# Split weights of a phase's first three units: general-pool buffers in pieces of 512 columns

## The chip, the cores and the metric

One core of a Trainium2 chip runs the whole kernel. The metric is the device time of one execution in microseconds (us); smaller is better.

## The reference, cut to what matters

Two layers of an encoder, 256 tokens, width 2048, float32. Each layer has a mixing phase and a feed-forward phase, each between two norms:

```
for l in range(DEPTH):                                   # DEPTH = 2
    h = rmsnorm(x, pre_mix_norm)
    proj = h @ w_in                                      # 2048 -> q/kv latents, conv, delta-net inputs
    o_a = attention(...);  o_b = convolution module(...);  o_c = gated delta net, both directions(...)
    x = x + rmsnorm(concat(o_a, o_b, o_c) @ w_out, post_mix_norm)
    h = rmsnorm(x, pre_ffn_norm)
    f = (silu(h @ w_gate) * (h @ w_up)) @ w_down         # 2048 -> 5632 -> 2048
    x = x + rmsnorm(f, post_ffn_norm)
```

All weights are read from memory once, some 400 MB, and nearly all the arithmetic is in the products with them.

## The kernel before, in words

**Products in three parts.** A float32 operand is split into a rounded half `hi` and the rest `lo = x - hi`, and a product is three matmuls: hi·hi, lo·hi, hi·lo. `hilo` (L327 to L329) makes the split: the cast on ScalarE (ACT, L328) and the subtraction on VectorE (DVE, L329). Both the tokens (on the left, moved into TensorE as 128x128 blocks) and the weights (on the right, 512 columns wide) are split.

**Units.** `dense` (L337) forms a product of 256 tokens, as two halves t = 0 and t = 1 of 128, with a weight block of `n` columns. Its weight rows come in units of two chunks of 128 rows. `unit(u)` loads 128x1024 floats into a buffer `ws` (5 of them, `WSB`), takes a pair of buffers `wh`, `wl` (5 pairs, `WHB`) and splits all 1024 columns with one cast and one subtraction. A unit has 6 matmuls for t = 0 (L353, L354, L355 for each chunk) and 6 for t = 1.

**Phase starts.** Each of the four phases (mixing and feed-forward, in two layers) begins with a `dense` call that has `head=HEADG=3`: the block "gq" of the mixing phase and the first gate block in `first_block`. Its tokens come from the phase's new `x`, which the end of the phase before makes last. So the first three units run their t = 0 matmuls alone, are kept in `held`, and their t = 1 matmuls follow together after unit 2. Until then the three pairs `wh`, `wl` are in use. A phase ends in `out_proj`, whose last `dense` has `tail=TAILG=4`: the last four units run t = 0 first, then t = 1, so that the sum, the norm and the residual of t = 0 (L1201, L1204, L1205, `rsqrt_sum` L257 to L270, four additions L495) run beside the t = 1 matmuls. These four units hold four of the five pairs.

**New tokens.** `norm_quad` transposes four 128x128 blocks of `x` on TensorE (L439, 32 transposes for both halves) and splits the result; the first group of t = 0 goes through `hilo_col` in four steps (L332, L333), the others through L448 and `hilo`.

**Order.** The program text is not the order of the queues. A planner places the instructions: it gives each engine, as soon as its model of that engine is free, the ready instruction that stands earliest in the text. Ready means that its inputs are there and that the buffer for its output is free. So an instruction that stands late in the text is put ahead of an earlier one that is still waiting. `hold` (L112, L492 to L497) limits that for the head units: the subtractions of units 1 and 2 may not be put ahead of the residual of t = 0 (`issue_after` orders within one engine, here VectorE; at the very first start the engine is ScalarE for units 1 and 2). It says nothing on units 3 and up.

**Pools.** `U()` gives a 128x512 buffer from the general pool (64 of them, `UB`), which holds all token data.

Of the kernel before, what the change touches and what calls it, by code (L numbers as in the profile page):

```python
# [10 lines left out]
F32R = mybir.dt.float32r  # L11
# [5 lines left out]
P = 128  # L17
# [25 lines left out]
WHB = 5  # L43
# [10 lines left out]
def kernel(  # L54
# [12 lines left out]
    wpool = ctx.enter_context(tc.tile_pool(name="wpool", bufs=3))  # L67
# [5 lines left out]
    def U(dt=F32):  # L73
        return upool.tile([P, 512], dt, tag="u", name="u")
# [252 lines left out]
    def hilo(hi, lo, src):  # L327
        act.copy(out=hi, in_=src)  # L328
        dve.tensor_tensor(out=lo, in0=src, in1=hi.bitcast(F32), op=ALU.subtract)  # L329
# [7 lines left out]
    def dense(lhs, ks, n, load, evac, ch=2, need=None, pre=None, head=0, mid=None, tail=0,  # L337
              after0=None):

        acc = [psa.tile([P, 512], F32, tag="acc", name="acc") for _ in range(NT)]
        nu = -(-len(ks) // ch)
        held = []

        def mm(t, c, u, kc, wh, wl):
            i = u * ch + c
            rh = wh[:, c * n:(c + 1) * n]
            rl = wl[:, c * n:(c + 1) * n]  # L350
            xh, xl = lhs(kc[c], t)
            o = acc[t][:, 0:n]
            pe.matmul(o, xh, rh, start=(i == 0), stop=False)  # L353
            pe.matmul(o, xl, rh, start=False, stop=False)  # L354
            pe.matmul(o, xh, rl, start=False, stop=(i == len(ks) - 1))  # L355

        def unit(u):
            kc = ks[u * ch:(u + 1) * ch]
            m = len(kc)
            ws = wpool.tile([P, 1024], F32, tag="ws", name="ws", bufs=WSB)  # L360
            wv = ws[:, 0:m * n].rearrange("p (c n) -> p c n", c=m)
            load(wv, kc[0], m)
            wh = wpool.tile([P, 1024], F32R, tag="wh", name="wh", bufs=WHB)
            wl = wpool.tile([P, 1024], F32R, tag="wl", name="wl", bufs=WHB)
            with ExitStack() as order:
                if u < head:
                    for u0, ins in hold:
                        if u >= u0:
                            order.enter_context(tc.issue_after(ins.ins))
                hilo(wh[:, 0:m * n], wl[:, 0:m * n], ws[:, 0:m * n])  # L370
            if need is not None:
                for k in kc:
                    bg.ensure(*need(k))
            return u, kc, wh, wl

        for u in range(nu):
            a = unit(u)
            if head <= u < nu - tail:
                for c in range(len(a[1])):
                    for t in range(NT):  # L380
                        mm(t, c, *a)
            else:
                for c in range(len(a[1])):
                    mm(0, c, *a)
                held.append(a)
                if u == head - 1 and mid is not None:
                    mid()
                if u == nu - 1:
                    if pre is not None:
                        pre()  # L390
                        pre = None
                    evac(0, acc[0][:, 0:n])
                if u in (head - 1, nu - 1):
                    for h in held:
                        for c in range(len(h[1])):
                            mm(1, c, *h)
                    held.clear()
            bg.step(BUDGET)
        if pre is not None:
            pre()  # L400
        if after0 is not None:
            after0()
        for t in range(1 if tail else 0, NT):
            evac(t, acc[t][:, 0:n])
# [1056 lines left out]
```

## Time and profile before

| what | value |
|---|---|
| median of 3 runs | 2233.1 us (2231.53 to 2233.45) |
| profiled execution, its own time | 2234.73 us |
| its span in the trace | 2233.0 us |
| mean granted TensorE clock | 0.998 of full speed |
| TensorE (PE) busy | 99% of the span |
| VectorE (DVE) busy | 79% |
| ScalarE (ACT) busy | 53% |

The profiled execution lies 1.6 us above the median, and 1.7 us of its time lie outside the span. Busy shares of PE count a matmul up to its modelled end, so waits of PE are read from the starts of successive instructions and not from the busy share.

### The profile page before, as it was taken

Reading aid. Unit: us, or ns where it says so; the run is one execution under the profiler, and the core shown is the slowest. Engines: PE = TensorE matmul, PEld = TensorE weight load, DVE = VectorE, ACT = ScalarE, POOL = GpSimd, SP = SyncE. Lnnn points to the kernel's source line nnn. Section 1 sums busy time; section 2 is a strip of 40 time slices with the busy share of each in tenths; the row PEclk is TensorE's granted clock in tenths of the full one; section 3 lists DMA queues with packets and bytes.
Section 4 is the critical chain, followed back from the end, with each engine's and each line's share of the span. In section 5 each row is a group of like instructions: output and inputs, shape, how many; then the busy total and the mean of one; then the engine's idle time right before and its main releaser. Section 6 shows DMA issues by size and latency. Waiting matters only on the chain.

```text
span 2233.0 us, 29215 instructions
## 1 busy us (share of the span) xinstructions
PE 2203.0 (99%) x10483; PEld 1839.3 (82%) x10483; DVE 1762.0 (79%) x2873; ACT 1182.5 (53%) x1642; POOL 45.9 (2%) x93
## 2 busy tenths in 40 slices
PE   8999999999999999999999999999999999999998
PEld 7988887788888888888879888877888888888886
DVE  6777998899999897544486779979999998975444
ACT  6665545555555555444356655455555555554432
POOL 2000000000000000000000000000000000000000
PEclk9999999999999999999999999999999999999999
DMA  7554525546656656555556545245565566665553
GB/s 254 171 178 146 188 89 162 162 164 207 217 181 217 225 189 223 171 195 192 179 172 186 183 142 171 97 153 161 188 207 208 191 215 214 202 214 178 191 196 124
DMA packets 218545, 407.75 MB, mean 183 GB/s; under 512 B 17607, under 2 KB 30065, under 8 KB 218400
## 3 DMA queue, kind: packets, MB, share of 16 engines
q1 hardware_dynamic: 215360, 397.72, 54.3%
q0 software_dynamic: 3008, 8.16, 1.3%
q8 instruction: 82, 1.34, 0.2%
q14 instruction: 63, 0.52, 0.1%
q10 hardware_dynamic: 32, 0.01, 0.0%
HBM read 402.94 MB, written 2.90 MB: 182 GB/s over the span
## 4 chain that ended last, share of the span: by engine, by line
PE 92%; DVE 5%; DMA 1%; issue 0%; ACT 0%; SPq 0%; DVEq 0%; ACTq 0%; POOLq 0%
PE acc L1306 19%; PE tp L1306 19%; PE acc L353 16%; PE acc L354 16%; PE acc L355 16%; DVE wl L329 1%; DVE xs L495 1%; PE tp L1230 1%; PE tp L1051 1%; DVE u L950 1%; DMA cd<-u 1%; PE tp L795 0%; PE tp L802 0%; PE tp L1022 0%; DMA xs<-in_x_dram 0%
## 5 line engine op out<-in xcount | busy, mean ns | idle before, releaser
L328 ACT CAST wh<-ws 128x1024 fp32r<-128x1024 f32 (+3 forms) x820 | 815.5, 1010 | 795.2 <-PE acc L354 409.6
L329 DVE TENSOR_TENSOR wl<-ws,wh 128x1024 fp32r<-128x1024 f32 (+3 forms) x820 | 942.1, 1170 | 336.2 <-ACT wh L328 332.2
L353 PE MATMUL acc<-wh,u 128*128 128x512 f32 (+2 forms) x1792 | 695.5, 389 | 0.4
L354 PE MATMUL acc<-wh,u 128*128 128x512 f32 (+2 forms) x1792 | 686.2, 383 | 3.5 <-DVE u L329 1.8
L355 PE MATMUL acc<-wl,u 128*128 128x512 f32 (+2 forms) x1792 | 685.6, 383 | 3.0 <-DVE wl L329 3.0
L354 PEld LDWEIGHTS acc<-wh,u 128*128 128x128 f32 x1792 | 337.5, 188 | 68.4 <-DVE u L333 4.1
L355 PEld LDWEIGHTS acc<-wl,u 128*128 128x128 f32 x1792 | 336.8, 188 | 68.1 <-DVE wl L329 5.8
L353 PEld LDWEIGHTS acc<-wh,u 128*128 128x128 f32 x1792 | 337.3, 188 | 62.3 <-ACT u L332 2.5
L1306 PE MATMUL acc<-wh,u 128*128 128x512 f32 x1220 | 376.4, 389 | 0.0
L1306 PE MATMUL tp<-wh,u 128*128 128x512 f32 x1220 | 375.8, 389 | 0.0
L1306 PEld LDWEIGHTS acc<-wh,u 128*128 128x128 f32 x1220 | 228.7, 188 | 47.9 <-DVE u L329 0.6
L1306 PEld LDWEIGHTS tp<-wh,u 128*128 128x128 f32 x1220 | 228.9, 188 | 47.6
L1306 PE MATMUL acc<-wl,u 128*128 128x512 f32 x610 | 237.4, 389 | 0.0
L1306 PE MATMUL tp<-wl,u 128*128 128x512 f32 x610 | 237.3, 389 | 0.0
L1306 PEld LDWEIGHTS acc<-wl,u 128*128 128x128 f32 x610 | 114.5, 188 | 23.7
L1306 PEld LDWEIGHTS tp<-wl,u 128*128 128x128 f32 x610 | 114.5, 188 | 23.7
L950 DVE SCALAR_TENSOR_TENSOR u<-u,cols 128x241 f32<-128x241 f32 (+14 forms) x240 | 101.0, 470 | 0.0
L1344 ACT CAST wh<-ws 128x1024 fp32r<-128x1024 f32 x60 | 63.0, 1050 | 28.4 <-PE tp L1306 12.8
L1345 DVE TENSOR_TENSOR wl<-ws,wh 128x512 fp32r<-128x512 f32 x60 | 41.1, 686 | 23.8 <-ACT wh L1344 21.8
L328 ACT CAST u<-u 128x512 fp32r<-128x512 f32 (+2 forms) x48 | 27.8, 587 | 38.2 <-DVE u L448 34.2
L1329 ACT ACTIVATE u<-u,sm 128x512 f32<-128x512 f32 x40 | 28.8, 724 | 34.6 <-DVE u L1376 24.4
L1351 DVE TENSOR_TENSOR ws<-ws 128x512 f32<-128x512 f32 x60 | 41.5, 692 | 2.0
(303 smaller groups left out, 1541.8 us busy)
## 6 DMA issues: line engine op xcount, KB each, us to landing
ws<-in_w_gate_dram SPq DMA_DIRECT2D x176, 512.0 KB, 5.0
ws<-in_w_up_dram SPq DMA_DIRECT2D x176, 512.0 KB, 4.8
ws<-in_w_down_dram SPq DMA_DIRECT2D x176, 512.0 KB, 3.6
ws<-in_w_in_dram SPq DMA_DIRECT2D x112, 512.0 KB, 4.3
ws<-in_w_out_dram SPq DMA_DIRECT2D x64, 512.0 KB, 3.7
ws<-in_w_ukv_dram SPq DMA_DIRECT2D x16, 512.0 KB, 3.7
ws<-in_w_uq_dram SPq DMA_DIRECT2D x16, 384.0 KB, 3.5
ws<-in_w_in_dram SPq DMA_DIRECT2D x10, 444.0 KB, 4.1
```

Of the source, the lines that this page charges most:

```text
L328: act.copy(out=hi, in_=src)
L329: dve.tensor_tensor(out=lo, in0=src, in1=hi.bitcast(F32), op=ALU.subtract)
L353: pe.matmul(o, xh, rh, start=(i == 0), stop=False)
L354: pe.matmul(o, xl, rh, start=False, stop=False)
L355: pe.matmul(o, xh, rl, start=False, stop=(i == len(ks) - 1))
L495: ins = dve.scalar_tensor_tensor(out=xv, in0=parts[(c, t)], scalar=r[:, 0:1], in1=xv, op0=ALU.mult, op1=ALU.add)
L950: dve.scalar_tensor_tensor(out=o, in0=i, scalar=wc, in1=o, op0=ALU.mult, op1=ALU.add)
L1306: pe.matmul(o, a, b, start=count[i] == 1, stop=count[i] == total[i])
L1329: act.activation(out=sg[t], in_=x, func=AF.Silu, scale=rfb[0][:, t:t + 1])
L1344: act.copy(out=wh, in_=wg)
L1345: dve.tensor_tensor(out=wl[:, 0:512], in0=b11, in1=wh[:, 0:512].bitcast(F32), op=ALU.subtract)
L1351: dve.tensor_tensor(out=b21, in0=b21, in1=b22, op=ALU.subtract)
```

## The change

In the first `head` units of a `dense` call (three, at the four phase starts) the split weights no longer take a pair `wh`, `wl`. Each chunk gets two buffers of the general pool and a split of its own, 512 columns wide: two casts and two subtractions for a unit where there was one of each. All other units keep the pair and the split of 1024 columns. `mm` now takes a list with a (hi, lo) pair for each chunk.

```
-        def mm(t, c, u, kc, wh, wl):
+        def mm(t, c, u, kc, w):
             i = u * ch + c
-            rh = wh[:, c * n:(c + 1) * n]
-            rl = wl[:, c * n:(c + 1) * n]
+            rh, rl = w[c][0][:, 0:n], w[c][1][:, 0:n]
...
-            wh = wpool.tile([P, 1024], F32R, tag="wh", name="wh", bufs=WHB)
-            wl = wpool.tile([P, 1024], F32R, tag="wl", name="wl", bufs=WHB)
             with ExitStack() as order:
                 if u < head:
                     for u0, ins in hold:
                         if u >= u0:
                             order.enter_context(tc.issue_after(ins.ins))
-                hilo(wh[:, 0:m * n], wl[:, 0:m * n], ws[:, 0:m * n])
+                if u < head:
+
+                    w = [(U(F32R), U(F32R)) for _ in range(m)]
+                    for c in range(m):
+                        hilo(w[c][0][:, 0:n], w[c][1][:, 0:n], ws[:, c * n:(c + 1) * n])
+                else:
+                    wh = wpool.tile([P, 1024], F32R, tag="wh", name="wh", bufs=WHB)
+                    wl = wpool.tile([P, 1024], F32R, tag="wl", name="wl", bufs=WHB)
+                    hilo(wh[:, 0:m * n], wl[:, 0:m * n], ws[:, 0:m * n])
+                    w = [(wh[:, c * n:(c + 1) * n], wl[:, c * n:(c + 1) * n]) for c in range(m)]
...
-            return u, kc, wh, wl
+            return u, kc, w
```

## Rows read from the trace of the kernel before

**Rows 1.** The page, part 1: busy us (share) and instructions of each engine.
```profile
PE 2203.0 (99%) x10483; PEld 1839.3 (82%) x10483; DVE 1762.0 (79%) x2873; ACT 1182.5 (53%) x1642; POOL 45.9 (2%) x93
```

**Rows 2.** The waits of PE: waiter, releaser, total us, times, longest.
```profile
PE acc L355 <- DVE wl L329: 3.0, 6, 1.0
```

**Rows 3.** The four phase starts as windows: length, busy us (instructions), clock, DMA share, GB/s.
```profile
0.00:16.00 16.00, 9.74 (x34) 7.25 (x34) 6.87 (x13) 6.81 (x11) 13.79 (x41) 1.00 0.90 283
399.40:416.20 16.80, 14.34 (x67) 9.18 (x65) 16.10 (x34) 4.78 (x10) 0.00 (x0) 1.00 0.41 125
1117.00:1132.50 15.50, 13.43 (x67) 9.34 (x66) 14.74 (x31) 4.86 (x11) 0.20 (x1) 1.00 0.48 136
1506.20:1522.90 16.70, 14.25 (x66) 9.14 (x65) 16.02 (x34) 4.78 (x10) 0.00 (x0) 1.00 0.41 127
```

**Rows 4.** The chain of waits, one steady run of matmuls: start us, us, count.
```profile
482.73 12.24 PE tp L1306 x54
```

**Rows 5.** Timeline of PE, feed-forward start of layer 0: start, us, [idle before, releaser].
```profile
399.48 1.27 PE L439 MATMUL tp<-ident,xs 128*128 128x128 f32 x10
...
405.68 0.50 PE L355 MATMUL acc<-wl,u 128*128 128x512 f32 x1 [0.95 <-DVE wl L329]
...
409.07 0.50 PE L355 MATMUL acc<-wl,u 128*128 128x512 f32 x1 [0.28 <-DVE wl L329]
...
411.01 0.50 PE L355 MATMUL acc<-wl,u 128*128 128x512 f32 x1 [0.27 <-DVE wl L329]
```

**Rows 6.** Timeline of DVE around the same start.
```profile
389.70 1.23 DVE L329 TENSOR_TENSOR wl<-ws,wh 128x1024 fp32r<-128x1024 f32 x1 [0.22 <-ACT wh L328]
390.84 1.29 DVE L1205 TENSOR_TENSOR u<-u 128x512 f32<-128x512 f32 x2
...
394.24 0.69 DVE L1201 TENSOR_TENSOR u<-u,acc 128x512 f32<-128x512 f32 x1 [1.79 <-PE acc L355]
...
396.32 0.21 DVE L262 TENSOR_SCALAR sm<-sm 128x1 f32<-128x1 f32 x1
...
398.11 2.75 DVE L495 SCALAR_TENSOR_TENSOR xs<-u,sm,xs 128x512 f32<-128x512 f32 x4
...
403.11 0.20 DVE L262 TENSOR_SCALAR sm<-sm 128x1 f32<-128x1 f32 x1
...
404.41 1.22 DVE L329 TENSOR_TENSOR wl<-ws,wh 128x1024 fp32r<-128x1024 f32 x1
...
410.88 2.74 DVE L495 SCALAR_TENSOR_TENSOR xs<-u,sm,xs 128x512 f32<-128x512 f32 x4
...
425.79 2.35 DVE L329 TENSOR_TENSOR wl<-ws,wh 128x1024 fp32r<-128x1024 f32 x2
```

**Rows 7.** Timeline of ACT around the same start.
```profile
395.59 2.24 ACT L328 CAST wh<-ws 128x1024 fp32r<-128x1024 f32 x2
398.13 1.06 ACT L328 CAST wh<-ws 128x1024 fp32r<-128x1024 f32 x1 [0.31 <-PE acc L354]
```

**Rows 8.** Timeline of DVE, mixing start of layer 1.
```profile
1112.50 0.69 DVE L1205 TENSOR_TENSOR u<-acc,u 128x512 f32<-128x512 f32 x1 [4.07 <-ACT u L1204]
...
1122.48 1.22 DVE L329 TENSOR_TENSOR wl<-ws,wh 128x1024 fp32r<-128x1024 f32 x1
```

**Rows 9.** Timeline of PE, mixing start of layer 1.
```profile
1124.43 0.50 PE L354 MATMUL acc<-wh,u 128*128 128x512 f32 x1 [1.16 <-DVE u L329]
```

**Rows 10.** Groups by line and shape: count, busy us, mean ns, idle before by releaser.
```profile
L329 DVE TENSOR_TENSOR wl<-ws,wh 128x1024 fp32r<-128x1024 f32 x720 | 862.3, 1222 | 314.4 <-ACT wh L328 312.2
...
L329 DVE TENSOR_TENSOR wl<-ws,wh 128x512 fp32r<-128x512 f32 x60 | 41.2, 687 | 8.5 <-ACT wh L328 6.9 <-PE acc L1306 0.8 <-PE tp L1306 0.6
L328 ACT CAST wh<-ws 128x512 fp32r<-128x512 f32 x60 | 37.0, 616 | 37.7 <-DMA ws<-in_w_up_dram 27.5 <-DVE wl L1345 2.8 <-PE tp L1306 2.6
```

**Rows 11.** Timeline of PE, start of the kernel.
```profile
8.71 0.79 PE L354 MATMUL acc<-wh,u 128*128 128x512 f32 x1 [0.38 <-DVE u L333]
...
11.83 1.54 PE L439 MATMUL tp<-ident,xs 128*128 128x128 f32 x6 [0.62 <-DMA xs<-in_x_dram]
```

## The prediction

> **What bounds the kernel now.** I read the page first: PE is busy 99% of the span, VectorE 79%, ScalarE 53% [rows 1]. So the time is the sum of PE's work and its waits, and only a shorter wait of PE can make the kernel faster: the change takes no matmul away. Then the waits of PE: the costliest that the change touches is the wait for a subtraction of weights, 3.0 us in six times [rows 2]. It and nearly all others lie at the phase starts, so I made a window of each [rows 3]. The granted clock is 1.00 in all four, so no term for the clock arises. In a steady run 54 matmuls start in 12.24 us, 0.227 us each [rows 4]; ten transposes take 1.27 us, 0.127 each [rows 5]. The second window has 67 PE instructions, which are the 32 transposes and so 35 matmuls: 35 x 0.227 + 32 x 0.127 = 12.0 us of work in 16.8. The third has 12.0 in 15.5, the fourth, with 34 matmuls, 11.8 in 16.7. PE thus loses 4.8 + 3.5 + 4.9 = 13.2 us at the three starts after the first, and that bounds any gain there: 0.6% of the time.
>
> Of the 35 matmuls 18 are t = 0 of the three head units. The other 17 are mostly units 3 and 4, t = 0: PE already goes past the held units while the tokens of t = 1 are missing. What delays these tokens is VectorE, which in the same windows is busy 16.1, 14.7 and 16.0 us [rows 3]: from the residual of t = 0 (from 398.11) to that of t = 1 (from 410.88) it has no gap, and the small steps of the second norm, which take 1.8 us when alone (396.32 to 398.11), take 7.8 us (403.11 to 410.88), because subtractions of weights and tokens were put between them [rows 6].
>
> **The change, part by part.** I work it out for the feed-forward start of layer 0 and carry it to the other two.
>
> *Two pieces instead of one.* A subtraction of 1024 columns takes 1.222 us, one of 512 takes 0.687, a cast of 512 0.616 [rows 10] against 1.06 [rows 7]. Back to back they overlap: two large subtractions end 2.35 us after the first began, so they start 1.13 apart; two instructions of 512 columns take 1.29, so 0.60 apart [rows 6]. A unit costs VectorE 2 x 0.60 - 1.13 = 0.07 us more; bounds are 0 and 2 x 0.687 - 1.222 = 0.15. For 12 head units that is 0.9 us, of which units 1 and 2 lie in the full stretch of VectorE: 0.14 us per start. ScalarE has room (4.8 busy of 16.8 us [rows 3]); its second cast costs nothing on the path.
>
> [...]
>
> What the pieces give back: PE's third matmul of a chunk needs only its own 512 columns. At 405.68 PE had waited 0.95 us for the subtraction that began at 404.41 and took 1.22 [rows 5, 6]; a piece is done 0.53 us sooner. At the mixing start it is the token splits of 128 columns that stand behind a whole subtraction, with the same 0.53 to be had. Bounds 0 and 0.95; I take -0.5 per start.
>
> *Five pairs free for units 3 and up.* Before, the tail of the phase before holds four pairs and unit 0 the fifth (its subtraction is at 389.70 [rows 6]). Units 1 to 4 get theirs as the tail's t = 1 matmuls end, with casts at 395.59 (two), 398.13 and one after [rows 7]. After the change units 0 to 2 are split as soon as their data is there, and the fifth pair goes to unit 3. Its subtraction takes the place of unit 0's, and VectorE is idle near it: 1.79 us before 394.24, and 4.07 us before 1112.50 at the mixing start [rows 6, 8]. So unit 3 leaves VectorE's full stretch, which gets 1.13 us shorter; PE's waits of 0.28 at 409.07 (unit 3) and of 0.27 at 411.01 (unit 4) go, and at the mixing start the wait of 1.16 at 1124.43, which stands behind unit 3's subtraction at 1122.48 [rows 5, 8, 9]. With the restart of PE behind each wait I take -0.9; bounds -1.2 and -0.5.
>
> *What is late next.* Unit 4 takes the first pair that the tail gives back. Its cast can begin at 395.59 and end at about 396.6, when the norm of t = 0 is at its first step (396.32). No order is set for unit 3 and up, so the planner can put this subtraction into that chain, as it did in the chain of t = 1 [rows 6]. Behind it on VectorE stand the rest of the chain and the four additions of the residual; behind them wait PE's transposes of the new tokens and everything after. PE has no other work there, since its tail ends at 399.48. Price: 0 if nothing is put in, 1.13 for one, 3.4 for three (units 4, 5, 6; pairs come back every six matmuls, 1.36 us). One is nearest to the row: +1.1. What PE loses there comes back in part, because units 4 to 6 are then ready and PE fills the waits before t = 1 with their t = 0 matmuls, 1.36 us a unit: of the small gaps left before 416 I take -0.4 (0 to -0.8).
>
> *Loads, general pool, first start.* Head units' `ws` buffers come free earlier by several us, so SyncE issues units 5 and 6 earlier; the transfers run at a DMA share of 0.41 to 0.48 at these starts [rows 3] and collide with nothing. The 12 general buffers are wanted while, by the text, at most some 55 of 64 are in use; if one had to wait, unit 2 would be as late as before: 0. At the first start VectorE's subtraction stands before the token split that PE waits 0.38 us for, but 3 us later PE waits for the input itself [rows 11]: what is gained is lost there, 0 (bounds -0.5 and +0.3).
>
> *Sum.* Per start -0.5 + 0.14 - 0.9 + 1.1 - 0.4 = -0.56; three give -1.7, and I put -2 with the first start's side. The profiled 2234.7 us would be 2232.7; the runs shown have their median at 2233.1, and the forecast goes against that: 2231.
>
> **The rivals.** *Full gain.* The planner puts nothing ahead of the residual of t = 0, and the early units fill PE's gaps. Then a start gains 0.5 + 0.9 + 0.8 and some of its remaining loss, about 2.2 to 2.5 us of the 3.5 to 4.9: 2226. For it: unit 4 becomes ready only 0.3 us after the chain's start, and the planner's model need not agree with the chip. Against it: every gap of the chain of t = 1 was filled.
>
> *Slower.* At each start the subtractions of units 4, 5 and 6 run between the steps of the norm of t = 0, each making it long enough for the next pair to come back. The residual is 3.4 us late, PE stands still for 2.7 of them (its first transposes have 0.7 us in hand: first addition done at 398.8, tail until 399.48), and unit 7 does the same to t = 1 with 1.1. Less 0.4 + 0.5 + 0.9 that is some +1.9 per start: 2239. It decides from the second subtraction put ahead of that residual. For it: chain of t = 1, 7.8 us instead of 1.8 [rows 6]. Against it: the subtractions done early are missing later, so the delay is largely paid back as long as PE then has units 5 and 6 to run.
>
> *Nothing gained.* VectorE's work before t = 1 is the same sum in another order, units 5 and 6 in place of 3 and 4, and PE's starts move by tenths: 2233.
>
> **How the numbers follow.** Forecast -2 with its own range 2228.6 to 2233: 0.45. Nothing, 2233 to 2235: 0.2. Full gain, 2224 to 2228.6: 0.2. Slower, 2235 to 2241: 0.15. The range 2225 to 2238 leaves out about one in ten on the two sides together, and a little more for reorderings that the planner makes far from the starts. A measurement of this kernel tells 0.2%, 4.5 us, from no change: below 2228.6 is faster, 0.22 (the full gain and the edge of the forecast); above 2237.6 slower, 0.13; the rest, 0.65, is the same.
>
> **What would show it.** Right: in the after trace 24 casts and subtractions of 512 columns write general buffers; unit 3's subtraction lies before the residual of t = 0 at each late start; the waits for `wl` at 409 and 411 are gone, that at 405.68 shrinks by half; one large subtraction stands between the steps of the first norm; more than 35 matmuls precede the first of t = 1. Wrong: that norm's steps take over 4 us with PE idle behind its tail (the slower rival), or under 2 us with a window shorter by over 2 us (full gain); or a difference outside the four windows larger than 2 us.

## The result, and the profile after

The changed kernel takes 2256.5 us (median of 5 runs, 2255.8 to 2258.9) against 2233.1: ratio 1.0105, 95% interval 1.009 to 1.012. It is slower by 23 us, where 2231 was forecast, with 2225 to 2238 as the range. The profiled execution has a span of 2254.3 us against 2233.0.

The page, part 1, answers to [rows 1]: PE has the same 10483 instructions, and VectorE and ScalarE each have the 12 more that the pieces bring, for 2.7 and 0.3 us of work.
```profile
PE 2205.7 (98%) x10483; PEld 1841.3 (82%) x10483; DVE 1764.7 (78%) x2885; ACT 1182.8 (52%) x1654; POOL 47.0 (2%) x93
```
PE's busy time is up by 2.7 us with the same instructions, so most of the 21 us more of span are waiting, not work. The waits of PE (waiter, releaser, total us, times, longest) answer to [rows 2]; lines below the diff are numbered 6 higher than before, and the three matmuls of a chunk (L353 to L355 before) are now L352 to L354.
```profile
PE acc L352 <- ACT u L328: 13.2, 6, 3.4
...
PE acc L354 <- DVE u L329: 4.5, 9, 0.9
PE tp L445 <- DVE xs L501: 4.4, 3, 1.9
```
The wait that the change was to shorten, for `wl`, is gone from the head of the list. In its place PE waits 13.2 us for *casts* into general buffers (L328 writing `u`), which the kernel before doesn't show, and 4.4 us for the residual of t = 0. The windows (length, PE busy and instructions, clock, DMA share, GB/s) of 40, 45 and 41 us from the three late starts, first of the kernel before, then of the changed one, show where:
```profile
396.00:436.00 40.00, 37.54 (x170) 1.00 0.47 140
1115.00:1160.00 45.00, 42.92 (x198) 1.00 0.54 164
1504.00:1545.00 41.00, 38.55 (x173) 1.00 0.50 153
```
```profile
396.00:436.00 40.00, 33.33 (x146) 0.91 0.42 121
1115.00:1160.00 45.00, 38.64 (x173) 0.96 0.44 129
1504.00:1545.00 41.00, 33.93 (x149) 0.92 0.51 156
```
In each stretch PE gets through 24 or 25 instructions fewer, at 0.227 us [rows 4] some 5.5 us, and the granted clock is under 1.00, where [rows 3] have 1.00.

Now the feed-forward start of layer 0 in detail. The timeline of ACT (start us, us, instruction, in brackets the idle time before it and its releaser) answers to [rows 7]:
```profile
393.26 1.05 ACT L328 CAST wh<-ws 128x1024 fp32r<-128x1024 f32 x1 [2.93 <-DMA ws<-in_w_gate_dram]
...
405.22 1.05 ACT L328 CAST wh<-ws 128x1024 fp32r<-128x1024 f32 x1 [4.01 <-DMA ws<-in_w_gate_dram]
406.18 0.36 ACT L332 ACTIVATE u<-tp,cols 128x128 fp32r<-128x128 f32 x1
...
408.51 0.62 ACT L1210 ACTIVATE u<-u 128x512 f32<-128x512 f32 x1
...
409.13 0.60 ACT L328 CAST u<-ws 128x512 fp32r<-128x512 f32 x1
...
412.81 0.62 ACT L328 CAST u<-u 128x512 fp32r<-128x512 f32 x1 [1.48 <-DVE u L454]
413.33 2.17 ACT L328 CAST u<-ws 128x512 fp32r<-128x512 f32 x4
```
The changed kernel is some 3.4 us behind here, from the kernel start and the mixing phase. Unit 3 is cast at 393.26, as the prediction had it. But unit 0's first piece (`u<-ws`) is cast only at 409.13, behind the sum of squares of t = 1 (L1210), and units 1 and 2 at 413.33, behind the cast of a group of tokens (`u<-u`). Before, unit 0's subtraction was done by 391 [rows 6]. ScalarE was not short of time: it stood idle for 4.01 us ahead of 405.22. The order of its instructions was another one. (That the data of unit 0 was missing can be left out: in `early` below, all six casts of units 0 to 2 run by 397.3.)

The timeline of DVE answers to [rows 6]:
```profile
399.71 0.20 DVE L262 TENSOR_SCALAR sm<-sm 128x1 f32<-128x1 f32 x1
...
400.27 1.22 DVE L329 TENSOR_TENSOR wl<-ws,wh 128x1024 fp32r<-128x1024 f32 x1
...
401.48 1.22 DVE L329 TENSOR_TENSOR wl<-ws,wh 128x1024 fp32r<-128x1024 f32 x1
...
403.98 2.74 DVE L501 SCALAR_TENSOR_TENSOR xs<-u,sm,xs 128x512 f32<-128x512 f32 x4
...
416.03 2.74 DVE L501 SCALAR_TENSOR_TENSOR xs<-u,sm,xs 128x512 f32<-128x512 f32 x4
```
The norm of t = 0 takes 4.3 us (399.71 to 403.98) instead of 1.8, with two subtractions of later units between its steps; the residual of t = 1 comes at 416.03 instead of 410.88, 5.2 us later, of which 3.4 were there before. And PE, answering to [rows 5, 9, 11]:
```profile
11.18 0.90 PE L445 MATMUL tp<-ident,xs 128*128 128x128 f32 x3 [3.60 <-DMA xs<-in_x_dram]
11.73 0.78 PE L352 MATMUL acc<-u 128*128 128x512 f32 x1
...
404.88 1.95 PE L445 MATMUL tp<-ident,xs 128*128 128x128 f32 x12 [1.85 <-DVE xs L501]
409.78 0.50 PE L352 MATMUL acc<-u 128*128 128x512 f32 x1 [2.96 <-ACT u L328]
...
411.06 0.63 PE L352 MATMUL acc<-u 128*128 128x512 f32 x1
411.49 0.63 PE L353 MATMUL acc<-u 128*128 128x512 f32 x1
...
414.00 0.79 PE L352 MATMUL acc<-u 128*128 128x512 f32 x1 [1.31 <-ACT u L328]
...
1131.38 0.79 PE L352 MATMUL acc<-u 128*128 128x512 f32 x1 [3.16 <-ACT u L328]
```
After the transposes PE stands still for 2.96 us until unit 0's first piece is cast; no other matmul of the phase runs ahead of it (in the text unit 0's first matmul has the `start` of the sum). After that wait matmuls start 0.43 us apart instead of 0.227 (from 411.06), and PE waits again at 414.00. The window of this stretch has a granted clock of 0.50, where [rows 3] have 1.00:
```profile
411.00:417.80 6.80, 5.22 (x11) 0.50 0.57 168
```
Mixing in layer 1 begins in the same way (3.16 us at 1131.38), and at the kernel start the first matmul with weights is at 11.73, behind the input, where it was under way before 8.71 [rows 11]. [Rows 8]: at the mixing start two subtractions stand ahead of the residual as well (1122.55 and 1123.79). [Rows 10]: nothing became slower by itself; the large subtraction takes 1221 ns, the pieces 690, their casts 613.

### The profile page after: what moved, and what is told of

Its sections match the earlier page's. It is cut to its first block, busy times and chain, and to the rows that moved or that the text cites. A ratio compares the mean times of both kernels' runs of the same rounds, so it can differ in the third digit from the quotient of the medians.

```text
span 2254.3 us, 29231 instructions
## 1 busy us (share of the span) xinstructions
PE 2205.7 (98%) x10483; PEld 1841.3 (82%) x10483; DVE 1764.7 (78%) x2885; ACT 1182.8 (52%) x1654; POOL 47.0 (2%) x93
## 3 DMA queue, kind: packets, MB, share of 16 engines
q8 instruction: 82, 1.34, 0.2%
## 4 chain that ended last, share of the span: by engine, by line
PE 92%; DVE 4%; DMA 2%; issue 1%; ACT 1%; SPq 0%; POOL 0%; DVEq 0%; ACTq 0%; POOLq 0%
PE tp L1312 18%; PE acc L1312 18%; PE acc L354 16%; PE acc L352 16%; PE acc L353 16%; DVE wl L329 1%; PE tp L1236 1%; DMA ws<-in_w_in_dram 1%; PE tp L1057 1%; DMA cd<-u 0%; PE tp L808 0%; PE tp L801 0%; PE tp L1028 0%; DVE u L956 0%; DMA ws<-in_w_gate_dram 0%
## 5 line engine op out<-in xcount | busy, mean ns | idle before, releaser
L328 ACT CAST wh<-ws 128x1024 fp32r<-128x1024 f32 (+4 forms) x808 | 802.7, 1009 | 808.8 <-PE acc L353 406.6
L329 DVE TENSOR_TENSOR wl<-ws,wh 128x1024 fp32r<-128x1024 f32 (+4 forms) x808 | 928.5, 1169 | 347.5 <-ACT wh L328 342.8
L352 PE MATMUL acc<-wh,u 128*128 128x512 f32 (+2 forms) x1744 | 675.6, 388 | 0.0
L353 PE MATMUL acc<-wh,u 128*128 128x512 f32 (+2 forms) x1744 | 665.5, 382 | 0.8 <-DMA ws<-in_w_in_dram 0.8
L354 PE MATMUL acc<-wl,u 128*128 128x512 f32 (+2 forms) x1744 | 665.4, 382 | 0.0
L354 PEld LDWEIGHTS acc<-wl,u 128*128 128x128 f32 x1744 | 327.4, 188 | 60.9
L353 PEld LDWEIGHTS acc<-wh,u 128*128 128x128 f32 x1744 | 328.1, 188 | 59.6 <-DVE u L329 2.0
L352 PEld LDWEIGHTS acc<-wh,u 128*128 128x128 f32 x1744 | 327.9, 188 | 58.0 <-ACT u L328 0.5
L1312 PEld LDWEIGHTS acc<-wh,u 128*128 128x128 f32 x1220 | 228.8, 188 | 47.4
L1312 PEld LDWEIGHTS acc<-wl,u 128*128 128x128 f32 x610 | 114.5, 188 | 23.9
L328 ACT CAST u<-u 128x512 fp32r<-128x512 f32 (+2 forms) x48 | 27.8, 587 | 43.0 <-DVE u L454 42.3
L329 DVE TENSOR_TENSOR u<-u 128x512 fp32r<-128x512 f32 (+2 forms) x48 | 30.8, 649 | 17.5 <-ACT u L328 17.5
```

Of the source, the lines that this page charges most:

```text
L1312: pe.matmul(o, a, b, start=count[i] == 1, stop=count[i] == total[i])
```

## The experiments

Two suspects showed in this trace: the late pieces of units 0 to 2, and the subtractions ahead of the residual. Why are the pieces late? My reading of the planner, which no trace records, is that the buffers of the general pool are given out strictly in the order of the text: tokens of group 0 (two), unit 0 (four), tokens of group 1 (three), unit 1 (four), unit 2 (four). A wh/wl pair has a queue of its own, in which the head was first. In the general pool the head's splits can get no buffer until the tokens of t = 0 ahead of them have theirs. The trace agrees with that order: unit 0's first cast (409.13) comes after the first split of new tokens (406.18), and those of units 1 and 2 (413.33) right after the cast of the next group (412.81). I call this theory 1 (order). Theory 2: the freed pairs let subtractions of units 3 to 5 in ahead of the residual of t = 0. Theory 3: the pieces themselves.

**First group: the three theories apart.** Of each kernel the edit, the expectation on record, and the result. `pieces` is the kernel before, with
```
-                hilo(wh[:, 0:m * n], wl[:, 0:m * n], ws[:, 0:m * n])
+                if u < head:
+                    for c in range(m):
+                        hilo(wh[:, c * n:(c + 1) * n], wl[:, c * n:(c + 1) * n], ws[:, c * n:(c + 1) * n])
+                else:
+                    hilo(wh[:, 0:m * n], wl[:, 0:m * n], ws[:, 0:m * n])
```


> The kernel before with one part of the change alone: units 0 to 2 are split in two casts and two subtractions of 512 columns, into the same wh/wl pairs as before, nothing in the general pool. Theory 1 (order: buffers of the general pool are handed out in the order of the text, so the head's splits wait behind token buffers): the pieces are innocent, 2230 to 2236, no more than 3 us from the kernel before. Theory 2 (subtractions of units 3 to 5, let go by the freed pairs, delay the residual of t = 0): no pair is freed here, the same 2230 to 2236. Theory 3 (24 small instructions in place of 12 large ones, and twice as many steps between engines, make the head slower by themselves): 2245 to 2256, most of the 23 us.

Measured: 2235.3 us, ratio 1.0007 (0.9998 to 1.0016). The pieces cost nothing that can be measured, and they give nothing: theory 3 is out.

`early` is the changed kernel with the buffers taken earlier in the text:
```
+    def take():
+        for _ in range(4 * HEADG):
+            w = U(F32R)
+            pool.memset(w[:, 0:1].bitcast(F32), 0.0)
+            taken.append(w)
...
-                    w = [(U(F32R), U(F32R)) for _ in range(m)]
+                    w = [(taken.pop(0), taken.pop(0)) for _ in range(m)]
...
         if l == 0:
+            take()
             norm_quad(0, 0, hT, (0, PRE_MIX))
...
+                    if last and nb == 3 and after0 is not None and not (rname == "rd" and l == DEPTH - 1):
+                        take()
                     dense(lhs, ks, 512, wload(w, nb * 512, 512), ev, need=need,
```


> The changed kernel, with the 12 general buffers of the head taken earlier in the text: ahead of the last projection of the phase before (at the kernel start ahead of the first tokens), each marked as taken by GpSimd writing one column of it. Everything else as changed: pieces, general pool, freed pairs. Theory 1 (order): unit 0 is split before the residual of t = 0 again, PE's wait of 3 us for its cast is gone, the clock stays up; what is left is the subtractions of units 3 to 5 ahead of that residual, 2 to 3 of 1.13 us at each of three starts: 2234 to 2242. Theory 2 (freed pairs): as the subtractions still stand ahead of the residual, most of the loss stays: 2248 to 2256. Theory 3 (pieces): 2245 to 2256.

Measured: 2240.1 us, ratio 1.0030 (1.0019 to 1.0042). 16.4 of the 23 us are gone, by holding the same buffers *longer*; that speaks against a shortage in the pool as well. The timeline of ACT now has all six casts of the head in one run, 15 us earlier:
```profile
394.08 3.21 ACT L328 CAST u<-ws 128x512 fp32r<-128x512 f32 x6
```
What is left is visible in the timeline of DVE, three subtractions in the norm of t = 0, and in that of PE, which waits for the residual behind them:
```profile
399.41 1.22 DVE L329 TENSOR_TENSOR wl<-ws,wh 128x1024 fp32r<-128x1024 f32 x1
...
400.62 1.22 DVE L329 TENSOR_TENSOR wl<-ws,wh 128x1024 fp32r<-128x1024 f32 x1
...
401.88 1.22 DVE L329 TENSOR_TENSOR wl<-ws,wh 128x1024 fp32r<-128x1024 f32 x1
...
404.12 2.74 DVE L501 SCALAR_TENSOR_TENSOR xs<-u,sm,xs 128x512 f32<-128x512 f32 x4
```
```profile
405.02 1.29 PE L445 MATMUL tp<-ident,xs 128*128 128x128 f32 x8 [3.56 <-DVE xs L501]
```
This is the slower rival of the prediction, in its place and in its total (2239 for three subtractions at each start).

`late_hold` leaves the buffers late and takes away the subtractions ahead of the residual:
```
-                if u < head:
+                if head and u < head + 3:
                     for u0, ins in hold:
```


> The changed kernel, with units 3, 4 and 5 also held until the residual of t = 0 has been issued, as units 1 and 2 are. The general buffers are still handed out late. Theory 1 (order): the residual comes 2.3 us earlier at each late start, but unit 0 still waits for token buffers: 3 x 2.3 = 7 us of the 23 at most come back, 2249 to 2254. Theory 2 (freed pairs): nearly all comes back, 2233 to 2240. Theory 3 (pieces): 2250 to 2258.

Measured: 2257.3 us, ratio 1.0105 (1.0091 to 1.0119). Nothing came back; theory 2 is out as the main cause, and theory 1 had allowed some gain, 2249 to 2254. PE's wait for unit 0's cast is what it was, and units 3 to 5 are now split beside units 0 to 2; the waits of PE in this kernel:
```profile
PE acc L352 <- ACT u L328: 13.5, 7, 3.4
PE acc L354 <- DVE u L329: 6.0, 11, 1.1
```
`early_hold` has both edits.

> Both edits on the changed kernel: the head's general buffers are taken early in the text, and units 3, 4 and 5 are held behind the residual of t = 0. Theory 1 with theory 2 as a smaller part: both losses are gone, and unit 0 is in pieces ahead of the residual: 2228 to 2235, at the kernel before or a little under it. If the two losses simply add, early and late_hold together give back what this one does. Theory 3 (pieces): 2245 or more, whatever the order.

Measured: 2235.1 us, ratio 1.0010 (1.0001 to 1.0019). In the windows of the starts PE has nearly the count of the kernel before, at clock 1.00:
```profile
396.00:436.00 40.00, 36.85 (x169) 1.00 0.47 147
1115.00:1160.00 45.00, 43.99 (x201) 1.00 0.54 164
1504.00:1545.00 41.00, 37.96 (x173) 1.00 0.49 155
```
The two losses do not add: the hold is worth 5.0 us when the buffers are early and nothing when they are late. While unit 0 is missing PE waits for it, whenever the residual comes.

**Second group: the clock, and what more buffers are worth.** In the windows of the starts the changed kernel had a granted clock of 0.91, 0.96 and 0.92, `early` one of 0.96 in all three. Is the clock a part of the loss? `early_warm` gives PE something to do where it stood still in `early`:
```
+    def busy(n, ins):
+        with tc.issue_after(ins.ins):
+            b = TP()
+            for _ in range(n):
+                pe.matmul(b, fill[:, 0:P], fill, start=True, stop=True)
...
+                            lastmm = mm(1, c, *h)
+                    if u == nu - 1 and tail and hold and after0 is not None and warm[0]:
+                        busy(12, lastmm)
```


> The kernel `early` (general buffers of the head taken early), with 12 matmuls of 128x512 on constants, whose result nobody reads, put on PE behind the last matmul of the tail at each of the three late starts: 2.7 us of work in the gap of 2.5 to 3.7 us in which PE waited for the residual of t = 0. In `early` each of these gaps was followed by a stretch at clock 0.5. Theory A (the clock: what remains of the loss in `early` is that PE ran at half clock after it had stood still; the late residual itself is paid back by the early units): the clock stays at 1.00 in the windows of the starts, and 1.5 to 1.7 us per start come back: 2234 to 2236. Theory B (the late residual itself costs): no change, 2239 to 2241.

Measured: 2239.9 us, ratio 1.0026 (1.0015 to 1.0037); the profiled execution alone was 2.3 us shorter than that of `early`; the medians of the timed runs are 0.2 us apart. The windows of `early`, then of `early_warm`:
```profile
396.00:436.00 40.00, 35.75 (x163) 0.96 0.43 142
1115.00:1160.00 45.00, 42.29 (x190) 0.96 0.43 131
1504.00:1545.00 41.00, 36.55 (x167) 0.96 0.45 141
```
```profile
396.00:436.00 40.00, 37.70 (x175) 1.00 0.42 133
1115.00:1160.00 45.00, 44.10 (x205) 1.00 0.46 142
1504.00:1545.00 41.00, 39.32 (x182) 1.00 0.41 132
```
The clock is at 1.00 now, as theory A said; but without the 12 fillers the counts are 163, 193 and 170, at most three more than in `early`, and no gain shows in the time. At full speed PE reached the next piece sooner and waited for it (1.34 us for a subtraction at 410.01): at the feed-forward start of layer 0, from the last matmul of the tail to the first of unit 3, PE took 12.3 us in both (401.07 to 413.40 in `early`, 400.21 to 412.48 here). Here the low clock was a consequence of waiting (0.96 with the gaps, 1.00 with them filled), and it took what would have been a wait anyway. Theory A falls with the size that it had, 1.5 to 1.7 us a start; the two intervals leave room for a smaller gain.

`after_warm` is the same on the changed kernel, with the 12 matmuls behind the transposes of t = 0 (`busy(12, tr)`).

> The changed kernel, with 12 matmuls of 128x512 on constants, whose result nobody reads, put on PE behind the transposes of t = 0 at each of the three late starts, where PE then waited 3.0 to 3.4 us for unit 0's cast. The waits for data stay; only the standing still before them is filled. By the windows of the starts of the changed kernel (clock 0.91 over 40 us, 0.96 over 45, 0.92 over 41) half clock took away 3.6 + 1.8 + 3.3 = 8.7 us. Theory A (clock): 6 to 9 us come back, 2247 to 2250. Theory B (the waits alone are the loss): 2255 to 2258, as the clock then only stretches work that would wait anyway.

Measured: 2258.6 us, ratio 1.0111 (1.0097 to 1.0124). The window at 396 still has a clock of 0.91: the matmuls 0.43 us apart came after the next wait (1.60 us at 416.72) instead, from 418.81 to 420.51. No time came back, but since the clock fell all the same, this kernel can't tell the two theories apart for the changed kernel.

`whb7` is the kernel before with `WHB = 7` and `UB = 56`.

> The kernel before with the memory moved for good: seven pairs of weight buffers instead of five (WHB 7), and 56 general buffers instead of 64 (UB 56, the same memory). No pieces, and the head's splits don't wait in the general pool's order. Theory 1 (the loss of the change comes from the order in which the general pool hands out): no loss here, 2229 to 2236; and if more buffers for the weights are worth anything at these starts, it is under 2230. Theory 2 (freed pairs let subtractions in ahead of the residual): 2238 to 2244.

Measured: 2235.5 us, ratio 1.0009 (1.0001 to 1.0018). With a queue of their own, more buffers for the weights bring no loss of the size of the change's; and by themselves they bring no gain. They let nothing into the norm of t = 0, so theory 2 is not tested by this kernel. Nor does unit 3 move ahead: between the two residuals VectorE still has four subtractions of weights (405.16, 406.37, 408.30 and 410.24).

`pool34` is the kernel before, with
```
+                if head and u in (3, 4):
+                    act.copy(out=wh[:, 0:m * n], in_=ws[:, 0:m * n])
+                    pool.tensor_tensor(out=wl[:, 0:m * n], in0=ws[:, 0:m * n], in1=wh[:, 0:m * n].bitcast(F32), op=ALU.subtract)
```


> The kernel before, with the subtractions of units 3 and 4 at the starts done by GpSimd instead of VectorE (an idle engine; its subtraction of 128x256 took 0.735 us in the kernel before, so by columns some 2.9 us for one of 128x1024). It tests what bounds the starts once the order is right: if VectorE's full stretch up to the residual of t = 1 does, the tokens of t = 1 come up to 2.3 us earlier at each of three starts, and the kernel is faster than before: 2226 to 2231. If GpSimd's longer subtraction is itself waited for by PE, or the starts are bound by the chain of the norm, 2231 to 2238.

Measured: 2244.5 us, ratio 1.0047 (1.0033 to 1.0061), slower than either end of what I expected. The timelines of POOL and of DVE in the same four microseconds say why:
```profile
397.29 2.47 POOL L372 TENSOR_TENSOR wl<-ws,wh 128x1024 fp32r<-128x1024 f32 x1 [140.43 <-ACT wh L371]
399.70 2.81 POOL L372 TENSOR_TENSOR wl<-ws,wh 128x1024 fp32r<-128x1024 f32 x1
```
```profile
397.45 2.85 DVE L499 SCALAR_TENSOR_TENSOR xs<-u,sm,xs 128x512 f32<-128x512 f32 x1
400.22 2.83 DVE L499 SCALAR_TENSOR_TENSOR xs<-u,sm,xs 128x512 f32<-128x512 f32 x1
```
Each of these additions of the residual has a median of 0.747 us over the kernel's 32. These two, begun while GpSimd subtracts, take 2.85 and 2.83 us, and each ends 0.5 us after the subtraction that it met. So this kernel tells nothing about VectorE as the bound; it moved work to an engine beside whose subtractions these additions took nearly four times as long. (The 0.735 us of the expectation is a multiplication's, L729 of the kernel before; GpSimd's eight subtractions of 128x1024 took 2.62 us at the median here.)

**Third group: which unit, and a faster order.** `late0` and `late12` are the changed kernel with `if head and u in (0,):`, or `(1, 2)`, in place of `if u < head:` ahead of the general buffers.

> A part of the change: only unit 0 of each head is split into the general pool in pieces (4 buffers); units 1 and 2 keep their wh/wl pairs. By theory 1 (order) unit 0's splits wait behind the token buffers of t = 0, as in the changed kernel. If the loss of the change is unit 0's lateness, this kernel shows most of it: 2246 to 2256. If it is the lateness of units 1 and 2, or the freed pairs (one instead of three here): 2233 to 2241.

> The other part: unit 0 keeps a wh/wl pair, units 1 and 2 go to the general pool in pieces (8 buffers, two pairs freed). Unit 0 is then split ahead of the residual of t = 0 as in the kernel before. If the loss is unit 0's lateness: 2234 to 2242 (what is left are units 1 and 2 behind the tokens of the first groups, and a subtraction or two ahead of the residual). If it is units 1 and 2: 2246 to 2256.

Measured: `late0` 2239.8 us, ratio 1.0026 (1.0015 to 1.0037); `late12` 2238.0 us, 1.0021 (1.0012 to 1.0030). For `late12` that is as expected; for `late0` it is a miss. I had thought that unit 0's lateness is most of the loss; it is 6.2 us alone, 4.4 for the others, and 23 for all three. In `late0` PE waits for unit 0 just the same:
```profile
404.01 0.50 PE L352 MATMUL acc<-u 128*128 128x512 f32 x1 [2.31 <-ACT u L328]
...
405.73 0.80 PE L354 MATMUL acc<-u 128*128 128x512 f32 x1 [0.98 <-DVE u L329]
...
407.60 0.63 PE L352 MATMUL acc<-wh,u 128*128 128x512 f32 x1
```
but at 407.60 it goes on into unit 1 (`wh`), and its next wait is one of 0.46 us at 410.52: while it waited for unit 0, units 1 to 3 had been cast (396.33 to 399.94) and the first of their subtractions done (402.62). The following table puts the same instruction of each trace beside the kernel before (how many us later it starts); each is the first of its line in the stage.

| instruction (start in the kernel before) | after | late_hold | early | early_hold | late0 | late12 |
|---|---|---|---|---|---|---|
| first copy of layer 0's output projection (311.3) | 3.3 | 4.1 | 1.8 | 1.1 | 0.8 | -1.4 |
| first block of gate and up done, layer 0 (491.0) | 8.5 | 11.3 | 3.4 | 1.7 | 1.6 | -0.8 |
| first copy of layer 1's output projection (1418.1) | 15.8 | 17.0 | 5.0 | 0.9 | 3.1 | 2.8 |
| first block of gate and up done, layer 1 (1597.8) | 21.2 | 24.2 | 6.5 | 1.1 | 5.6 | 3.4 |
| end of the span (2233.0) | 21.2 | 24.2 | 6.6 | 1.0 | 5.7 | 3.4 |

Read down a column: the changed kernel loses in all four phases, 3.3, 5.2, 7.3 and 5.4 us, and nowhere after the last start. The first and the third of these also hold something that lies far from the starts. The last stretch of a mixing phase, from its last projection (L1062, L1068 in the changed kernel) to the first copy, has 206 or 207 PE instructions; these are its windows in layers 0 and 1, first of the kernel before, then of the changed one:
```profile
272.00:311.30 39.30, 37.66 (x207) 0.96 0.32 108
1380.40:1418.10 37.70, 36.06 (x206) 1.00 0.34 113
```
```profile
277.00:314.70 37.70, 36.06 (x207) 1.00 0.35 112
1394.50:1433.90 39.40, 37.59 (x206) 0.96 0.32 108
```
The clock fell there once in each kernel, in layer 0 before and in layer 1 after, and that stretch is 1.6 or 1.7 us longer than its like. Read at the start of these stretches instead, the changed kernel loses 4.9, 5.2, 5.6 and 5.4 us, nearly the same in each phase; of the 4.9 of the first, `pieces` and `whb7` have 1.9 as well (274.0 in both). The -1.4 of `late12` arises there too (at its last projection it is at 272.2, the kernel before at 272.1).

`late0` and `late12` lose little at the first two starts. My reading is that a unit that comes late is paid back as long as the others are ready when it comes; with all three late, one wait follows another, and nothing pays. No run shows this by itself: why three late units cost 23 us where one costs 6.2 and two 4.4 stays open.

`whb7_t1` and `early_all_t1` try to use what was learnt: all three head units split ahead of the residual of t = 0, and fewer subtractions between the two residuals. On `whb7`, and the same on `early`:
```
-                if u < head:
+                if head and u < head + 3:
...
-            hold[:] = [(1, ins)]
+            hold[:] = [(3, ins)]
+        else:
+            hold.append((4, ins))
```


> A try at a faster kernel from `whb7` (seven private pairs, 56 general buffers): units 0, 1 and 2 may be split as soon as their data is there, unit 3 is held behind the residual of t = 0, units 4 and 5 behind the residual of t = 1. Between the two residuals VectorE then has one subtraction of weights instead of four. If VectorE's full stretch bounds the starts, the tokens of t = 1 come up to 3.4 us earlier, of which PE can use what it lacks in ready units: 1 to 2 us per start, 2227 to 2232. If what is done earlier is missing later (units 4 and 5 then come late): 2233 to 2240.

> The same order of holds on the changed kernel with its buffers taken early (`early`): units 0 to 2 in pieces in the general pool as soon as their data is there, unit 3 behind the residual of t = 0, units 4 and 5 behind that of t = 1. Against `whb7_t1` it tells pieces in the general pool from private pairs under the same order: by theory 1 nothing but the order matters, so within 3 us of `whb7_t1`.

Measured: `whb7_t1` 2231.8 us, ratio 0.9993 (0.9984 to 1.0001); `early_all_t1` 2233.7, 0.9998 (0.9989 to 1.0007). Within 3 us of each other, as theory 1 said, and neither told apart from the kernel before. In its profiled execution `early_all_t1` has the general pool, the pieces and no loss at any start, 3.4 us ahead of the kernel before at the end; the 11 timed runs spread from 2230.0 to 2236.7 and don't bear a gain out. In both kernels, at each of the three late starts, one subtraction of weights is left between the two residuals; at the feed-forward start of layer 0, where there were four, the residual of t = 1 follows that of t = 0 after 9.7 and 10.0 us instead of 12.8. So shortening VectorE's full stretch by some 3 us a start, which the prediction took to delay the tokens of t = 1, gave back 3.6 us at most over the whole kernel (the lower end of the first interval).

## Why the prediction was wrong

The step that failed is in "Loads, general pool, first start": the general buffers were costed at 0, since at most some 55 of 64 are in use. No run speaks against the count, but I asked whether there is a free buffer, not who is served first; and the one delay that I thought of was unit 2's. Measured, this term is 16.4 us (changed kernel against `early`), and it took down the sentence on which the gains stood, "units 0 to 2 are split as soon as their data is there": unit 0's subtraction was at 389.70 [rows 6], and after the change its cast alone is at 409.13. (For units 1 and 2 that sentence was wrong by the text alone: `hold` keeps their subtractions behind the residual of t = 0, in `early` too.)

- *Pieces*, +0.14 and -0.5 a start: both within what can't be measured (`pieces`, +1.6 us by the ratio, with an interval of -0.4 to +3.6). PE's waits for `wl` stay as in [rows 2]. The half subtraction is done sooner, but VectorE has the same work ahead of it.
- *Five pairs free*, -0.9 a start: unit 3 did move ahead of the residual (cast at 393.26, subtraction at 394.35). No run has this term alone: in `whb7` unit 3's subtraction stays between the residuals, and in `early_hold` it is held there (409.53). The nearest are `whb7_t1` and `early_all_t1`, which take three subtractions out of VectorE's full stretch; they gain 1.6 us (interval -0.2 to +3.6) and 0.4 (-1.6 to +2.5) over all starts. So no gain of the size forecast shows, and the term's size stays open. The restart of PE that it counts in was an estimate; in the kernel before, the matmuls that end the three waits at 405.68, 409.07 and 411.01 are followed by the next after 0.34, 0.35 and 0.34 us instead of 0.227.
- *What is late next*, +1.1 a start for one subtraction: there were two in the changed kernel and three in `early`. The mechanism was right and the number of instructions too small. Its price is the difference between `early` and `early_hold`, 5.0 us or 1.7 a start, and the rival that was worked out for three (+1.9 a start, 2239) meets `early` at 2240.1. That the totals meet so closely is partly luck: the rival's sum takes off gains of 1.8 a start that no run shows one by one, and PE stood still for 3.56 us (405.02 in `early`) where it had 2.7. But in the changed kernel this term shows as nothing (`late_hold`), since PE waits for unit 0 anyway.
- *First start*, 0 (bounds -0.5 and +0.3): 4.9 us of delay in the changed kernel by the end of the projections (272.1 against 277.0), 1.8 with the buffers early (273.9 in `early`). The trace has the same order there: weights behind tokens, and tokens behind the input.
- *No term for the clock*: the clock did fall, to 0.85 in the window 399.4 to 416.2 of [rows 3]. `early_warm` shows, for the order of `early`, no gain from keeping it up; for the changed kernel it stays open.
- *Other side*: the slower rival had its mechanism and sign, with a chance of 0.15, but its range ended at 2241. Its sign was even met in the changed kernel (the norm's steps took 4.3 us, with PE idle for 1.85), though its mechanism isn't most of the loss there. No rival had the head itself late, and the range had no bound for that: the cost of the pool was put at 0 with no upper end, from a count of buffers and not from a row.

Of the 23.5 us between the changed kernel and the runs of the kernel before beside these, then: 16.4 the time at which the head gets its general buffers, 5.0 the subtractions ahead of the residual once that is mended, 2.1 what remains, at the edge of what can be told from nothing.

## What to carry to other kernels

A buffer pool that several users share hands over its order together with its memory: before moving a tile into another pool, write down who stands ahead of it there and what those wait for, not only how many buffers are free. If the memory is to be shared, take the buffers in the text at the place where they are wanted first; if not, a small queue of their own is as good (`whb7`). And look for idle time on the engine that is waited for (4.01 us of ScalarE ahead of 405.22): work that is late on an engine with time to spare may be a matter of order.

## What the runs showed of the hardware

Beside subtractions on GpSimd, VectorE's additions of the residual were held up: in `pool34` such an addition, 0.747 us at the median, took 2.85 and 2.83 us beside subtractions of 2.47 and 2.81 us on GpSimd, and each ended about 0.5 us after the subtraction that it met. By what mechanism, no run shows.

And a low clock did not always cost time: in `early` PE ran some matmuls 0.43 us apart after it had stood still for 3.56 us, with a clock of 0.96 in the windows; filling the gap kept the clock at 1.00 in all three, and the medians stayed within 0.2 us (ratios 1.0030 and 1.0026, each with an interval of some 0.0011 to either side). Elsewhere it went with a loss: the last stretch of a mixing phase, with 206 or 207 PE instructions, took 39.3 and 39.4 us at a clock of 0.96 and 37.7 at 1.00.
